# A decoder layer on one core: both feed-forward blocks as seven products of half-size blocks, the down projection in three passes

## The chip, the cores and the metric

One Trainium2 chip, one of its cores. The engines are TensorE (PE; its weight loads are listed as PEld), VectorE (DVE), ScalarE (ACT), GpSimd (POOL) and SyncE (SP, which here only issues DMAs). The metric is the device time of one execution in microseconds (us). The kernel before has three timed runs: 1122.57, 1123.95 and 1125.03 us, median 1123.95.

## The reference

One layer of a decoder, 512 tokens of 1024 float32 features. Cut to what matters:

```python
def swiglu(x, wg, wu, wd):
    return (jax.nn.silu(x @ wg) * (x @ wu)) @ wd

h = h + 0.5 * swiglu(rmsnorm(h, ffn1_norm), ffn1_wg, ffn1_wu, ffn1_wd)
...
h = h + 0.5 * swiglu(rmsnorm(h, ffn2_norm), ffn2_wg, ffn2_wu, ffn2_wd)
gate = sigmoid(rmsnorm(h, ple_gate_norm) @ ple_w_gate)
h = h + gate * rmsnorm(p @ ple_w_proj, ple_norm)
```

Between the two feed-forward blocks stand a projection, two attention mixers and an output projection. `wg` and `wu` are 1024 x 2816, `wd` is 2816 x 1024. All weights are float32.

## The kernel before, in words

**Numbers in two parts.** TensorE multiplies float32r, which holds fewer digits than float32. So each operand is kept as two float32r parts, `hi` (a ScalarE copy) and `lo` (VectorE: the source minus `hi`), and each product of K tile by K tile is three matmuls (`passes`, L443): hi hi, hi lo, lo hi. Weights are loaded raw into a tile `st` and split by `split` (L355) into the tiles `hi` and `lo`.

**A feed-forward block** is `ffn` (L536). The 22 tiles of 128 hidden units go in chunks of 8, 7 and 7. In a chunk, gate and up of one tile take 8 K tiles x 3 matmuls each of 128 x 512 (hidden units by all 512 tokens), with the weights as the stationary operand; `hidden` (L449) makes silu(gate) x up and splits it. Then the chunk's rows of `wd` are multiplied for each half of 512 output columns and each of the 4 token tiles, and the sum is added to `h` with one VectorE op per token tile and half. That is 22 x 48 = 1056 matmuls for gate and up and 22 x 24 = 528 for down, in each block.

**The first block's start** is `ffn_start` (L471): the first two hidden tiles go K tile by K tile as `x` arrives, on a not yet normalized, transposed x; `rms_rows` (L517) then makes 1/rms as a row, and `hidden` multiplies gate by that row. The other tiles follow at once on the same `xT`. In the second block, `norm_tok` (L423) norms and transposes each token tile as it is finished, and the products of the embedding (`embedding`, L1153) stand between.

**What sets the order.** The program is recorded by `Plan` and issued by a list schedule (`issue`, L206): each engine takes, of the recorded instructions that are ready by the planner's cost estimates (`cost`, L107), the earliest. All instructions are therefore of line L296 in the profile (`emit`), and are told apart by their tiles. Each engine runs its list strictly in order. Tiles of a tag share a fixed number of slots (`Tag`); a tile of most tags (`x8`, `pt`, `k4`, `hi`, `lo`, `st`) gets a slot only in program order; `w2`, and the PSUM tags `acc` and `gub`, may go ahead. All loads and stores of size are issued by SP's queue. A cost is estimated from an instruction's engine, operation and size.

**Names in the profile.** `gub` and `acc` are PSUM banks (4 each), `w` is a `w2` tile of 512 columns, `k` a `k4` tile of 1024, `x` an `x8` tile of 2048, `pt` one of 1664; `hl`, `s`, `r` and `cs` are small tiles of the mixing.

Of the kernel before, what the change touches and what calls it, by code (L numbers as in the profile page):

```python
# [20 lines left out]
K4 = 14  # L21
# [33 lines left out]
class Plan:  # L55
    """Records the program and issues it in the order of a list schedule: each engine takes, of the
    instructions whose operands and slots are there, the one that stands first in the program."""
# [25 lines left out]
    def box(self, ap):  # L83
        """The partitions and, as a bit mask, the words of each partition that ap covers."""
# [104 lines left out]
    def weave(self, *streams, weights=None):  # L189
        """Records the streams side by side, in step by their work on the tensor engine."""  # L190
# [15 lines left out]
    def issue(self):  # L206
# [14 lines left out]
        def slot(op):  # L221
            """When the new tiles of op can have their slots; None if not yet known."""
# [14 lines left out]
        while done < len(ops):  # L237
# [18 lines left out]
            if best is None:  # L256
                raise RuntimeError("schedule stuck at " + str(oldest))
# [41 lines left out]
class Layer:  # L299
# [18 lines left out]
    def w2(self, shape=(P, 512), dt=F32):  # L318
        return self.nc.tile(self.sb, shape, dt, "w2", 8, 3)
# [7 lines left out]
    def act(self, m):  # L327
        """[128, 2, 512]: the two parts of one tile of hidden units, the m-th of its chunk."""
        if m < 4:
            return self.pt()[:, :1024].rearrange("p (a c) -> p a c", a=2)  # L330
        return self.k4((P, 2, 512), F32R)

    def pt(self):
        return self.nc.tile(self.sb, (P, 1664), F32R, "pt", 4)

# [19 lines left out]
    def split(self, st, a, n, gain=None, step=0, lo_engine=None):  # L355
        """st [128, a, n] as its two float32r parts."""
# [15 lines left out]
    def gain_columns(self, names, after=()):  # L372
        """Gains as columns, [128, K tiles] each."""
# [19 lines left out]
    def rstd(self, ss, n, cols=1):  # L393
        """(ss / n + eps) ** -0.5"""
# [10 lines left out]
    def transposed(self, srcs, dst_hi, dst_lo, gain=None):  # L405
        """Up to four [128, 128] blocks transposed, times their gain columns, and split into the two parts."""
# [31 lines left out]

    def new_xT(self):
# [8 lines left out]

    def hidden(self, m, pg, pu, R):  # L449
        """silu(gate * R) * up, in two parts."""  # L450
        nc = self.nc
        sg, a32 = self.w2(), self.w2()
        if R is not None:
            nc.vector.tensor_mul(sg, pg, R)
            pg = sg
        nc.scalar.activation(sg, pg, AF.Silu)
        nc.vector.tensor_mul(a32, sg, pu)
        at = self.act(m)
        nc.scalar.copy(at[:, 0], a32)
        nc.vector.tensor_sub(at[:, 1], a32, at[:, 0].bitcast(F32))  # L460
        return at[:, 0], at[:, 1]
# [881 lines left out]
```

## Time and profile before

| what | value |
|---|---|
| timed runs | 1122.57, 1123.95, 1125.03 us |
| median | 1123.95 us |
| span of the profiled execution, first to last instruction | 1122.3 us |
| instructions in the profile | 15134 |
| DMA over the span | 106.60 MB, mean 95 GB/s |

The profile is one execution. The page gives its span alone and no time of its own around it; the median of the timed runs is 1.65 us above the span. Busy time of an engine is the union of its instructions' records. Matmuls are pipelined, so one record (some 390 ns for 512 columns) is longer than the distance from one matmul to the next; a rate is read from the start of a run to its end, divided by the number of matmuls. In a timeline, instructions of one kind that follow each other are merged to one row with their count (x2) and their length together; a bracket tells how long the engine was idle before, and what ended that.

### The profile page before, as it was taken

The page shows a single profiled execution, that of the slowest core. Times are in us where ns is not written, and L with a number is a line of the kernel's source. Part 1 is how long each engine was busy: PE and PEld are TensorE (multiplying, and loading weights), DVE is VectorE, ACT ScalarE, POOL GpSimd, SP SyncE. Part 2 cuts the span into 40 slices and gives each one's busy share as a digit, 9 for nine tenths or more (in the row PEclk, how much of TensorE's full clock was granted, in tenths as well). Part 3 has the DMA queues.
Part 4 walks back from the last instruction along what each step waited for, and adds up shares of the span by engine and source line. Part 5 has one row for each costly group of instructions (what it writes and reads, how often), then busy time and mean ns, then how long its engine had stood idle before and what let it go on. Part 6 is the DMA issues. An engine that isn't in the chain of part 4 may idle for free.

```text
span 1122.3 us, 15134 instructions
## 1 busy us (share of the span) xinstructions
PE 1106.8 (99%) x5635; PEld 941.9 (84%) x5635; DVE 587.6 (52%) x1121; ACT 493.9 (44%) x1017; POOL 161.7 (14%) x312
## 2 busy tenths in 40 slices
PE   9999999999999999999999999999999999999998
PEld 6888888888888988898999888888888888888887
DVE  5443343334443687889889887733333323333353
ACT  5332132222321767978988964522222221222252
POOL 2000000000000167553344511200000000000010
PEclk9999999999999999999999999999999999999999
DMA  7432333333343631312102232433223323332221
GB/s 215 123 97 94 94 94 95 100 88 112 95 107 84 213 119 39 76 30 58 36 25 72 100 125 73 137 103 102 94 75 113 94 85 103 104 103 85 90 80 66
DMA packets 143657, 106.60 MB, mean 95 GB/s; under 512 B 12624, under 2 KB 125296, under 8 KB 143584
## 3 DMA queue, kind: packets, MB, share of 16 engines
q1 hardware_dynamic: 143392, 105.55, 31.3%
q8 instruction: 45, 0.74, 0.3%
q14 instruction: 28, 0.23, 0.1%
q0 software_dynamic: 192, 0.08, 0.1%
HBM read 101.29 MB, written 4.33 MB: 94 GB/s over the span
## 4 chain that ended last, share of the span: by engine, by line
PE 87%; DVE 4%; POOL 2%; ACT 2%; issue 2%; DMA 1%; SPq 0%; POOLq 0%; ACTq 0%
PE gub L296 49%; PE acc L296 39%; DVE k L296 1%; POOL s L296 1%; ACT w L296 1%; DVE w L296 1%; POOL r L296 1%; POOL w L296 1%; ACT k L296 1%; DVE s L296 1%; DVE lo L296 0%; DMA st<-in_w_in 0%; DVE x L296 0%; DMA spill<-k 0%; DMA ident<-in_ident 0%
## 5 line engine op out<-in xcount | busy, mean ns | idle before, releaser
L296 PE MATMUL gub<-x,hi 128*128 128x512 f32 x1376 | 424.7, 390 | 0.0
L296 ACT CAST hi<-st 128x1024 fp32r<-128x1024 f32 (+4 forms) x171 | 166.1, 981 | 502.4 <-PE acc L296 181.6
L296 PEld LDWEIGHTS gub<-x,hi 128*128 128x128 f32 x1376 | 258.3, 188 | 53.1
L296 DVE TENSOR_TENSOR lo<-st,hi 128x1024 fp32r<-128x1024 f32 (+4 forms) x171 | 192.6, 1134 | 194.4 <-ACT hi L296 189.7
L296 PE MATMUL gub<-x,lo 128*128 128x512 f32 x688 | 267.8, 389 | 0.0
L296 PE MATMUL acc<-hi,x 128*128 128x256 f32 (+3 forms) x720 | 181.9, 329 | 0.0
L296 PE MATMUL acc<-hi,k 128*128 128x512 f32 (+1 forms) x512 | 166.0, 391 | 2.2 <-DVE k L296 2.0
L296 PEld LDWEIGHTS gub<-x,lo 128*128 128x128 f32 x688 | 129.2, 188 | 26.9
L296 POOL TENSOR_SCALAR s<-s 128x1 f32<-128x1 f32 (+3 forms) x65 | 18.6, 286 | 801.6 <-ACT k L296 755.9
L296 PEld LDWEIGHTS acc<-hi,x 128*128 128x128 f32 x720 | 123.3, 190 | 5.2
L296 PE MATMUL acc<-hi,pt 128*128 128x512 f32 x384 | 122.4, 395 | 0.0
L296 PE MATMUL acc<-lo,x 128*128 128x256 f32 (+3 forms) x360 | 117.5, 328 | 0.0
L296 PEld LDWEIGHTS acc<-hi,k 128*128 128x128 f32 x512 | 96.7, 190 | 19.8 <-issue 2.2
L296 PE MATMUL acc<-lo,k 128*128 128x512 f32 (+1 forms) x272 | 103.2, 383 | 0.0
L296 DVE TENSOR_TENSOR w<-w,gub 128x512 f32<-128x512 f32 x42 | 28.9, 688 | 135.6 <-PE gub L296 135.6
L296 PEld LDWEIGHTS acc<-hi,pt 128*128 128x128 f32 x384 | 72.3, 188 | 16.9
L296 PE MATMUL acc<-lo,pt 128*128 128x512 f32 x192 | 75.7, 394 | 0.0
L296 PEld LDWEIGHTS acc<-lo,x 128*128 128x128 f32 x360 | 68.2, 190 | 2.7
L296 ACT ACTIVATE w<-w,s 128x128 f32<-128x128 f32 (+1 forms) x96 | 53.8, 563 | 9.7 <-DVE s L296 9.3
L296 PEld LDWEIGHTS acc<-lo,k 128*128 128x128 f32 (+1 forms) x272 | 50.0, 184 | 8.5
L296 PE MATMUL gub<-ident,w 128*128 128x128 f32 (+2 forms) x316 | 52.4, 274 | 0.6 <-ACT w L296 0.2
L296 POOL TENSOR_TENSOR s<-s,mhalf 128x1 f32<-128x1 f32 (+3 forms) x61 | 49.4, 810 | 4.1
(154 smaller groups left out, 1198.9 us busy)
## 6 DMA issues: line engine op xcount, KB each, us to landing
st<-in_ffn_wg SPq DMA_DIRECT2D x42, 512.0 KB, 3.8
st<-in_ffn_wu SPq DMA_DIRECT2D x42, 512.0 KB, 3.9
st<-in_ffn_wd SPq DMA_DIRECT2D x40, 512.0 KB, 3.6
st<-in_w_in SPq DMA_DIRECT2D x48, 128.0 KB, 2.5
st<-in_w_in SPq DMA_DIRECT2D x8, 512.0 KB, 3.8
st<-in_w_out SPq DMA_DIRECT2D x8, 512.0 KB, 3.8
st<-in_ple_w_gate SPq DMA_DIRECT2D x8, 512.0 KB, 3.9
k<-in_x SPq DMA_DIRECT2D x16, 128.0 KB, 4.1
```

The lines of the kernel that those rows point to most:

```text
L296: getattr(getattr(self.nc, op.eng), m)(*a, **k)
```

## The change

Gate and up, for two hidden tiles at a time (a pair), are a product of a 2 x 2 block matrix of weights (K halves by hidden tiles) with a 2 x 2 block matrix of x (K halves by token halves). The change computes it with seven products of half-size blocks instead of eight, after Strassen and Winograd: sums of blocks of x are made once per block in `x_operands`, sums of blocks of the weights for every pair in `gate_up`. Each of the seven products is 2 (gate, up) x 4 K tiles x 3 = 24 matmuls of 128 x 256. The first pair of the first block is still done as before. The hidden units stay in `k4` tiles, 11 of them.

The down projection comes after all pairs, and it too has seven products, 66 matmuls of 128 x 512 each; they don't fit in PSUM together, so it goes over all pairs three times: products 5, 6 and 4, then 1, 7 and 3, then product 2, whose sum goes on in the banks of product 1. Tokens 256 to 511 are finished after the second pass, 0 to 255 after the third, and the stages behind take the token tiles in the order 2, 3, 0, 1. The embedding's result, which stood in `x8` tiles through the second block, is written to DRAM and loaded again at the end.

The diff, cut to its core (V is VectorE, G is GpSimd):

```diff
-K4 = 14
+K4 = 17
+W2 = 9
...
-            return f * max(m / 1.2, self.cols(outs[0]) / 2.4) + 2.5
+            return f * max(m / 1.2 + 2.5, self.cols(outs[0]) / 2.4 + 13.5)
...
+        XR = [self.pt().bitcast(F32)[:, :1024].rearrange("p (k c) -> p k c", k=2) for _ in range(NK // 2)]
...
+            nc.gpsimd.tensor_tensor(XR[kp], xT[kp][0].bitcast(F32), xT[kp][1].bitcast(F32), ALU.add)
...
+    def two_parts(self, hi, lo, src):
+        nc = self.nc
+        nc.scalar.copy(hi, src)
+        nc.vector.tensor_sub(lo, src, hi.bitcast(F32))
+
+    def x_operands(self, XR, row=None):
...
+        if row is not None:
+            for x in XR:
+                for i in range(2):
+                    G.tensor_tensor(x[:, i], x[:, i], row, ALU.mult)
...
+                y = self.x8((P, 2, 4, 256))
+                hi, lo = y[:, 0], y[:, 1]
+            for n, a in enumerate(halves):
+                self.two_parts(hi[:, 2 * n:2 * n + 2], lo[:, 2 * n:2 * n + 2], a)
...
+        B = lambda r, c: [XR[2 * r + n][:, :, 256 * c:256 * c + 256] for n in range(2)]
...
+        sub(V, T3, B(1, 1), B(0, 1))
+        sub(G, T, B(0, 1), B(0, 0))
+        operand(7, T3)
+        operand(5, T)
+        sub(G, T, B(1, 1), T)
+        operand(6, T)
+        operand(1, B(0, 0))
+        sub(G, T, B(1, 0), T)
+        operand(4, T)
+        operand(2, B(1, 0))
+        operand(3, B(1, 1))
...
+    def gate_up(self, p, X, wg, wu):
...
+        for n, (r, c) in enumerate(((0, 0), (1, 0), (1, 1), (0, 1))):
+            t = self.st() if n % 2 else self.pt().bitcast(F32)[:, :1024]
...
+        s3 = self.pt().bitcast(F32)[:, :1024].rearrange("p (g k c) -> p g k c", g=2, k=4)
+        G.tensor_tensor(flat(s3), flat(q[0, 0]), flat(q[1, 0]), ALU.subtract)
+        w7 = operand(s3)
+        s = q[1, 0]
+        V.tensor_tensor(flat(s), flat(s), flat(q[1, 1]), ALU.add)
+        w5 = operand(s)
+        rc, rb, rd, r1 = self.gub(), self.gub(), self.accb(), self.accb()
+        product(7, w7, rc, True, False)
+        G.tensor_tensor(flat(s), flat(s), flat(q[0, 0]), ALU.subtract)
+        w6 = operand(s)
+        product(5, w5, rb, True, False)
+        p5 = self.w2()
+        nc.scalar.copy(p5, rb)
+        c22 = self.w2()
+        V.tensor_tensor(c22, p5, rc, ALU.add)
+        w1 = operand(q[0, 0])
+        product(6, w6, rd, True, True)
+        V.tensor_tensor(flat(s), flat(q[0, 1]), flat(s), ALU.subtract)
+        w4 = operand(q[1, 1])
+        product(1, w1, r1, True, False)
+        z = self.w2()
+        nc.scalar.copy(z, r1)
+        V.tensor_tensor(z, z, rd, ALU.add)
+        V.tensor_tensor(c22, c22, z, ALU.add)
...
+    def down(self, h, acts, wd, on_token):
...
+        steps = [range(a, min(a + 2, n)) for a in range(0, n, 2)]
...
+        b5, b6, b4 = [[f(), f()] for f in (self.accb, self.accb, self.gub)]
+        for st in steps:
...
+                w = self.x8((P, 4, 512), F32)
+                nc.sync.dma_start(w[:].rearrange("p (a d) c -> p a d c", a=2), raw(p))
+                G.tensor_tensor(w[:, 1], w[:, 1], w[:, 0], ALU.subtract)
+                V.tensor_tensor(w[:, 3], w[:, 3], w[:, 1], ALU.subtract)
+                G.tensor_tensor(w[:, 2], w[:, 2], w[:, 3], ALU.subtract)
...
+                G.tensor_tensor(s[:, 0], a[:, 2], a[:, 3], ALU.add)
+                G.tensor_tensor(s[:, 1], s[:, 0], a[:, 1], ALU.subtract)
+                o = act_op(3)
+                self.two_parts(o[:, 0, 0:2], o[:, 1, 0:2], s)
+                self.two_parts(o[:, 0, 2], o[:, 1, 2], a[:, 3])
+                V.tensor_tensor(a[:, 2], a[:, 1], a[:, 2], ALU.subtract)
+                V.tensor_tensor(a[:, 3], a[:, 0], s[:, 1], ALU.subtract)
+                acs.append(o)
+            for i, (banks, slot) in enumerate(((b5, 1), (b6, 3), (b4, 2))):
+                w = operands([x[:, slot] for x in ws])
+                for tt in range(2):
+                    product(banks, acs, i, w, first, last, tt)
+        for tt in range(2):
+            t = self.w2()
+            nc.scalar.copy(t, b5[tt])
+            V.tensor_tensor(t, t, b6[tt], ALU.add)
+            add(2 + tt, 0, b6[tt])
+            add(2 + tt, 0, b4[tt])
+            add(tt, 1, t)
+            add(2 + tt, 1, t)
...
+                G.tensor_tensor(w[:, 1], w[:, 2], w[:, 1], ALU.subtract)
...
+                self.two_parts(o[:, 0], o[:, 1], acts[p][:, 1:4])
...
+            nc.scalar.copy(t, b1[tt])
+            V.tensor_tensor(u, t, b7[tt], ALU.add)
+            add(2 + tt, 0, u)
+            add(2 + tt, 1, u)
+            on_token(2 + tt)
+            V.tensor_tensor(t, t, b3[tt], ALU.add)
+            add(tt, 1, t)
...
-    xT = L.new_xT()
+    XR = [L.pt().bitcast(F32)[:, :1024].rearrange("p (k c) -> p k c", k=2) for _ in range(NK // 2)]
...
     next(emb)
+    X = L.x_operands(XR)
     next(emb)
-    e = next(emb)
+    spilled, e_r = next(emb)
```

`norm_raw`, new, is `norm_tok` with plain copies of the transposed parts to `XR` in place of the split.

## Rows read from the trace of the kernel before

**Rows 1.** The page: busy time of each engine; its busy tenths in 40 slices.

```profile
PE 1106.8 (99%) x5635; PEld 941.9 (84%) x5635; DVE 587.6 (52%) x1121; ACT 493.9 (44%) x1017; POOL 161.7 (14%) x312
...
POOL 2000000000000167553344511200000000000010
```

**Rows 2.** Chain of waits in order of time: start, length, what.

```profile
100.05 44.09 PE acc L296 x192
144.13 76.17 PE gub L296 x336
...
704.74 4.78 PE acc L296 x21
```

**Rows 3.** Stretches: length, busy PE, PEld, DVE, ACT, POOL, clock, DMA share, GB/s.

```profile
402.00:406.00 4.00, 3.54 (x18) 3.57 (x19) 4.00 (x11) 1.95 (x5) 3.57 (x6) 0.61 0.05 14
5.00:10.00 5.00, 5.00 (x18) 3.07 (x17) 2.17 (x4) 2.58 (x5) 0.00 (x0) 1.00 0.98 316
144.00:220.00 76.00, 76.00 (x337) 62.96 (x336) 31.43 (x35) 21.73 (x27) 0.00 (x0) 1.00 0.33 100
```

**Rows 4.** Timeline of PE in the projections: start, length, operation, out<-in, shape, count.

```profile
396.18 0.28 PE L296 MATMUL acc<-lo,x 128*128 128x256 f32 x1
...
400.13 0.28 PE L296 MATMUL acc<-lo,x 128*128 128x256 f32 x1
402.46 0.35 PE L296 MATMUL acc<-hi,k 128*128 128x256 f32 x1 [2.05 <-DVE k L296]
```

**Rows 5.** Groups by line and form: count, busy us, mean ns, idle before.

```profile
L296 DVE TENSOR_TENSOR lo<-st,hi 128x1024 fp32r<-128x1024 f32 x134 | 163.6, 1224 | 184.0 <-ACT hi L296 179.2
L296 ACT CAST hi<-st 128x1024 fp32r<-128x1024 f32 x134 | 140.8, 1054 | 474.1 <-PE acc L296 172.3 <-PE gub L296 158.1 <-issue 139.0
L296 DVE TENSOR_TENSOR lo<-st,hi 128x512 fp32r<-128x512 f32 x16 | 10.6, 686 | 1.9 <-ACT hi L296 1.9
L296 DVE TENSOR_TENSOR w<-w,s 128x256 f32<-128x256 f32 x8 | 3.5, 438 | 2.6 <-POOL s L296 2.5
L296 POOL TENSOR_TENSOR w<-w 128x256 f32<-128x256 f32 x16 | 11.3, 705 | 16.8 <-ACT w L296 16.8
L296 POOL TENSOR_TENSOR x<-x,w 128x512 f32<-128x512 f32 x8 | 10.4, 1303 | 19.3 <-DVE w L296 14.5 <-PE gub L296 4.8
L296 POOL TENSOR_TENSOR r<-w,sin 128x16 f32<-128x16 f32 x24 | 7.9, 348 | 0.0
```

**Rows 6.** Timelines of DVE and POOL in the mixing, three places.

```profile
404.24 0.28 DVE L296 TENSOR_TENSOR k<-w,k 128x128 fp32r<-128x128 f32 x1
405.32 1.28 DVE L296 TENSOR_TENSOR lo<-st,hi 128x1024 fp32r<-128x1024 f32 x1
405.48 1.42 POOL L296 TENSOR_TENSOR r<-w,sin 128x16 f32<-128x16 f32 x2
...
539.20 1.29 POOL L296 TENSOR_TENSOR x<-x,w 128x512 f32<-128x512 f32 x1
539.49 1.22 DVE L296 TENSOR_TENSOR pt<-gub,pt 128x512 fp32r<-128x512 f32 x3 [0.36 <-ACT pt L296]
...
622.45 1.28 POOL L296 TENSOR_TENSOR x<-x,w 128x512 f32<-128x512 f32 x1 [0.18 <-DVE w L296]
622.95 0.93 DVE L296 TENSOR_TENSOR k<-w,k 128x128 fp32r<-128x128 f32 x1
```

**Rows 7.** Timelines of DVE, PE and ACT at the start of block one.

```profile
8.58 1.29 DVE L296 TENSOR_TENSOR lo<-st,hi 128x512 fp32r<-128x512 f32 x2 [0.21 <-ACT hi L296]
...
33.77 0.77 PE L296 MATMUL acc<-ident,w 128*128 128x128 f32 x5
34.69 0.58 ACT L296 COPY k<-acc 128x512 f32<-128x512 f32 x1
```

**Rows 8.** Timeline of DVE at the start of block two: the last token's parts.

```profile
705.22 1.28 DVE L296 TENSOR_TENSOR x<-gub,x 128x512 fp32r<-128x512 f32 x2
```

More of the change, by code (lines that the diff above doesn't have):

```diff
@@ L256, in issue @@
             if best is None:
-                raise RuntimeError("schedule stuck at " + str(oldest))
+                o = ops[oldest]
+                raise RuntimeError(f"schedule stuck at {oldest}: {o.eng} {o.call[0]} {o.tiles} "
+                                   + str({n: (len(t.free), t.queue[t.head:t.head + 2]) for n, t in self.tags.items()}))
             t, op = best
@@ new lines, in pair_tile, with operand, product, hidden @@
+    def pair_tile(self):
+        return self.k4((P, 4, 256))
+    def gate_up(self, p, X, wg, wu):
+        nc = self.nc
+        V, G = nc.vector, nc.gpsimd
+        q = {}
+        for n, (r, c) in enumerate(((0, 0), (1, 0), (1, 1), (0, 1))):
+            t = self.st() if n % 2 else self.pt().bitcast(F32)[:, :1024]
+            q[r, c] = t.rearrange("p (g k c) -> p g k c", g=2, k=4)
+            for i, w in enumerate((wg, wu)):
+                view = w[512 * c:512 * c + 512, (2 * p + r) * P:(2 * p + r + 1) * P]
+                nc.sync.dma_start(q[r, c][:, i], view.rearrange("(k p) c -> p k c", p=P))
+        flat = lambda x: x.rearrange("p g k c -> p (g k c)")
+        def operand(src):
+            hi, lo = self.hilo((P, 2, 4, P))
+            self.two_parts(flat(hi), flat(lo), flat(src))
+            return hi, lo
+        def product(i, w, bank, first, last):
+            for g in range(2):
+                for k in range(4):
+                    for n, (a, b) in enumerate(self.passes([x[:, g, k] for x in w], [x[:, k] for x in X[i]])):
+                        nc.tensor.matmul(bank[:, 256 * g:256 * g + 256], lhsT=a, rhs=b,
+                                         start=(first and g == k == n == 0), stop=(k == 3 and n == 2),
+                                         skip_group_check=True)
+        s3 = self.pt().bitcast(F32)[:, :1024].rearrange("p (g k c) -> p g k c", g=2, k=4)
[22 more added lines that the diff above has]
+        V.tensor_tensor(c22, c22, z, ALU.add)
+        acts = self.pair_tile()
+        def hidden(c, slot):
+            sg = self.w2()[:, :256] if c.space == PSUM else c[:, 0:256]
+            nc.scalar.activation(sg, c[:, 0:256], AF.Silu)
+            V.tensor_tensor(acts[:, slot], sg, c[:, 256:512], ALU.mult)
+        hidden(c22[:], 3)
+        w2 = operand(q[0, 1])
+        product(4, w4, rc, False, True)
+        c21 = self.w2()
+        V.tensor_tensor(c21, z, rc, ALU.add)
+        hidden(c21[:], 0)
+        w3 = operand(s)
+        product(2, w2, r1, False, True)
+        hidden(r1[:], 1)
+        product(3, w3, rb, False, True)
+        c12 = z
+        V.tensor_tensor(c12, z, rb, ALU.add)
+        hidden(c12[:], 2)
+        return acts
@@ L621, in mix_consts, with project @@
         self.lf = c("lf", (P, NT, 8))
-    def project(self, xT, groups, done, name):
+    def project(self, xT, groups, done, name, order=range(NT)):
         nc, d = self.nc, self.d
@@ L638, in project @@
         yield
-        for t in range(NT):
+        for t in order:
             ps = self.accb()
@@ L1164, in embedding @@
         yield
-        es, ss = [], [self.small(2) for _ in range(NT)]
+        spill = [self.dram.tile([P, NT, 512], F32, name=f"spill_e{half}") for half in range(2)]
+        ss = [self.small(2) for _ in range(NT)]
         for half in range(2):
             w = self.wcols(wp, 0, half)
-            e = self.x8((P, NT, 512), F32)
-            es.append(e)
             for t in range(NT):
@@ L1182, in embedding @@
             nc.gpsimd.tensor_tensor(s1, ss[t][:, 0:1], ss[t][:, 1:2], ALU.add)
-            r = self.rstd(s1, D)
-            for half in range(2):
-                e = es[half][:, t]
-                nc.vector.scalar_tensor_tensor(e, e, r, g[:, half * 512:half * 512 + 512], op0=ALU.mult, op1=ALU.mult)
-        yield es
+            r.append(self.rstd(s1, D))
+        yield spill, r
 @with_exitstack
@@ L1201, in layer @@
     w1 = d["ffn1_wg"][0], d["ffn1_wu"][0]
[L1202 to L1203 removed]
+    XR, started = L.ffn_start(x, h, L.gcol["ffn1_norm"], *w1)
+    row = L.rms_rows(h)
+    X = L.x_operands(XR, row)
+    first = L.started_acts(started, row)
     spill = [L.dram.tile([P, D], F32, name=f"spill{t}") for t in range(NT)]
     L.gain_columns(["mix_norm", "ple_gate_norm", "out_norm_nsa", "out_norm_fox"], [L.started])
[L1206 removed]
+    aT, a_r = [], [None] * NT
     def to_mix(t):
@@ L1282, in layer @@
     ks = [L.xk(gT[0], k) for k in range(NK)]
+    e = [L.x8((P, NT, 512), F32) for _ in range(2)]
+    ge = gain("ple_norm")
     for half in range(2):
+        nc.sync.dma_start(e[half], spilled[half])
+        for t in range(NT):
+            nc.vector.scalar_tensor_tensor(e[half][:, t], e[half][:, t], e_r[t], ge[:, half * 512:half * 512 + 512],
+                                           op0=ALU.mult, op1=ALU.mult)
         w = [L.wcols(wg, kp, half, L.gcol["ple_gate_norm"]) for kp in range(4)]
-        for t in range(NT):
-            step = 256 if half and t == NT - 1 else 512
+        for t in (2, 3, 0, 1):
+            step = 256 if half and t == 1 else 512
             for c in range(0, 512, step):
```

219 lines of the change are left out of this document (128 added, 91 removed).

## The prediction

> **What bounds the kernel now.** I read the share of busy time per engine first: TensorE is busy for 1106.8 of 1122.3 us, VectorE for half the span, and POOL (GpSimd) for 161.7 us [rows 1]. The slices say where: POOL has work at the start and in the middle (the mixing) and shows 0 in the stretches of the two feed-forward blocks [rows 1]. The chain of waits is there one run of products after another, each beginning where the last ends [rows 2]: 192 products of 512 columns in 44.09 us in a down projection, or 229.6 ns each, and in gate and up 336 in 76.17 us, or 226.7 ns. A table of stretches shows what lies beside the products of gate and up: VectorE 31.43 of 76 us, ScalarE 21.73, POOL nothing, DMA busy a third [rows 3]. So TensorE bounds both blocks, and only fewer columns, or the same columns faster, can gain there; whatever else gets slower than TensorE takes its place.
>
> **What the change takes away.** A product of 256 columns is not in the blocks now, but in the projections: from 396.18 to 400.13 us stand 33 of them, 119.7 ns each [rows 4]; I use 120. Gate and up: the first block keeps its first two tiles as they are, so 20 + 22 tiles change. Before, 42 x 48 = 2016 products x 226.7 ns = 457.0 us; after, 21 pairs x 168 = 3528 x 120 = 423.4 us; 33.6 us less. Down: 7/8 of 528 products in each block, 132 fewer in both, x 229.6 ns = 30.3 us less. Together **63.9 us less TensorE work**. In the rows a product takes its columns at 2.4 GHz plus 13.4 ns. [...]
>
> **What it adds.** Each operand of a product must be summed and then split into two parts. The prices: the split of 1024 columns costs ScalarE 1.05 and VectorE 1.22 us, of 512 VectorE 0.69; a 256-column op costs VectorE 0.44; POOL takes 0.70 for 256 and 1.30 for 512 [rows 5]. POOL at 1024 is not in the trace: at least 1.30, at most four times the 256 row, 2.8; the step from 256 to 512, 0.60, continued gives 2.5, which I take.
>
> These engines are not independent. While VectorE made a 1024-column split from two SBUF tiles (405.32 to 406.60), POOL's 16-column op, begun at 405.48, and the next one were not done until 406.90, though the group's mean is 348 ns. At 622.45 it is the other way: POOL's 512-column sum runs to 623.73, and VectorE's 128-column op on two SBUF tiles, begun at 622.95, ends at 623.88, 0.93 us for what the same op takes in 0.28 at 404.24. At 539.20 POOL's sum ran beside three VectorE ops that read PSUM, and these took their usual time [rows 6]. So a POOL sum and a VectorE op with both inputs in SBUF **take turns**. [...] It speaks against this change, which gives POOL sums of SBUF tiles where it had none, beside splits that all read two SBUF tiles. So I add the times of the two engines wherever both work from SBUF.
>
> *Gate and up, per pair.* VectorE: 9 ops of 1024 (7 splits, 2 sums), 5 sums of 512, 4 products of 256. By means 9 x 1.22 + 5 x 0.69 + 4 x 0.44 = 16.2 us; back to back (two 512 splits in 1.29, so the second adds 0.60 [rows 7]) nearer 15. POOL: 2 x 2.5 = 5. Four of the 512 sums and one 256 product read PSUM and may run beside POOL. That is 19.9 to 21 us against 168 x 0.12 = 20.2 us of TensorE: just about full. ScalarE has 7 x 1.05 + some 3 = 10. Loads are 2 MB a pair as before. I take 0.4 us a pair: **8 us** (0 to 20).
>
> *Down, first pass, per pair.* TensorE: 18 x 0.2296 = 4.13 us. VectorE: 5 ops of 512 and 3 of 256, all from SBUF: 4.8 by means, 4.1 back to back. POOL: 2 of 512 and 2 of 256: 4.0, or 3.2 if a waiting op's fixed part hides. In turns: 7.3 to 8.8; I take the middle, 8.0, twice TensorE's need. Eleven pairs: 88 us. Ahead of the pass TensorE is still in the last gate-and-up pair, where the weights of up to six pairs may be loaded as the `x8` tiles come free, the first after 1/7 of that pair's 20 us; a load of 1 MB needs over 3 us at the 316 GB/s that the trace shows at full share [rows 3], and the pair's own last splits stand in the queue, so I take that 8 us of this work go before (0 to 12). 88 - 8 - 11 x 4.13 = 34.6: **34 us a block** (23 to 46), 68 in both.
>
> *Pass two:* VectorE 3 splits of 512 and one of 768, POOL one 512 sum: about 4.1 us a pair, level with TensorE. But VectorE enters it late and with 2 x 5 evacuation ops (512 columns, as 0.69) ahead of the new operands in its queue: **7 us a block** (4 to 16), 14. *Pass three:* no POOL sums; VectorE has 2 x 5 evacuation ops, the 4 splits of two tokens' norms and 11 pairs x (0.69 + 0.44), some 7 + 3 + 12 = 22 us against 66 x 0.23 = 15.2, part of it done before: **5 us a block** (2 to 8), 10.
>
> *Start of block one.* Now the products of the third tile follow the first two at once. After the change everything must first become an `x_operands` tile. The row of 1/rms is there at 35.3 (transposes at 33.77 behind the first products, ScalarE's copy at 34.69 [rows 7]). Then POOL multiplies 8 x 1.30 = 10.4: 45.7. The new pair's third `pt` tile, `s3`, needs a slot that an `XR` tile holds until the sums for operands 7, 6 and 4 and the split for 2 have read it, and the `x8` tiles go in strict order, so 7, 5, 6, 1 and 4 come before 2: POOL 5 x 1.30 and VectorE 12 x 0.69 in turns, 14.8: 60.5. Then the other half on POOL 1.3, `s3` 2.5, its split 1.05 + 1.22, and hand-overs: about 67.3, against the end of the transposes at 34.5 [rows 7]. **33 us** (20 to 40; at the low end the engines overlap), and no other product is in reach. q00 and q11 load meanwhile, once operand 1 is split.
>
> *Start of block two.* The same from the last token's parts, now ready at 706.5 [rows 8], without the multiplications: 5 x 1.30 + 13 x 0.69 = 15.5, then 1.3 + 2.5 + 2.3: 728. The embedding's products cover TensorE until 709.5 [rows 2]. 18 us; the first half of that work can begin with the first tiles: **16 us** (5 to 22).
>
> *Clock.* After an idle 2.05 us before 402.46 [rows 4] the granted clock of 402 to 406 is 0.61 [rows 3], against 1.00 elsewhere: some 3.1 of 4 us at the lower level, 1.2 GHz, half of which is lost, 1.5 us. Two long idles and some in the passes: **4 us** (3 to 10).
>
> *At nothing:* the stores of e (8 x 256 KB) and its later load; SP's queue has room, DMA moves under a third of the time in the blocks [rows 3], against 316 GB/s at full share there. Its eight multiplications move from the second block's start to the end, where VectorE waits for products; if that cover fails, 8 x 0.69 = 5.5 us. Loads in pass one, 11.5 MB in 80 us, are 144 GB/s. The new token order (2, 3, 0, 1) lets the project and the gate begin on finished tokens while 0 and 1 are normed. The planner's new costs reorder the mixing: 0, within 5 either way.
>
> **Sum.** 8 + 68 + 14 + 10 + 33 + 16 + 4 = 153 added, 63.9 removed: 1122.3 + 89.1 = 1211.4 for the span. The page gives the profiled execution's span alone; the median of the runs is 1.65 above it and I take that as what lies around: **1213 us**.
>
> **Rivals.** (a) *Sharing costs nothing, faster.* If POOL's sums ran beside VectorE's, pass one would ask 4.8 of VectorE and 4.0 of POOL against 4.13: 6 us a block with the evacuations; gate and up would fit; the starts would be 26 and 12, as their chains still wait in turn for slots; clock 3. 53 - 63.9 = 11 less: 1113. It decides at a first pass of 4.13 us a pair. Against it stand both blocked ops of [rows 6]; for it, that these are narrow ops. Chance 0.09. (b) *The sharing costs its low end,* 7.3 a pair with 12 us done ahead (23 a block), gate and up level, starts 25 and 10, passes two and three 8 a block, clock 3: 100 added: 1160. Chance 0.15. (c) *Gate and up fall behind too:* 1 us a pair (21) and pass one at 8.8 without a head start longer than 8 (43 a block), the rest as forecast (77): 184 added: 1244. Chance 0.12. (d) The sums of (a) and (b) mix to no change; 0.02. That the change doesn't do what it says is excluded on TensorE by the 120 ns.
>
> **Chances.** The forecast has 0.62, and its own range is 1180 to 1245. With (b) and most of (c): 1150 to 1255. Faster by over 0.2% (2.2 us, about what a measurement of this kernel can tell) 0.09, within it 0.02, slower 0.89.
>
> **What would show it.** In the profile after: POOL busy in the blocks; VectorE's 512 splits in pass one longer than 0.69 in the mean, as each waits for a POOL sum; TensorE's busy share of pass one near a half, waiting for VectorE's `lo`; an idle TensorE of some 30 us after the first products and 16 at the second block's start; a gate-and-up pair every 20.2 to 21 us. The prediction is wrong if pass one takes less than 6 us a pair, or if products of the first new pair begin before 50 us.

## The result, and the profile after

The changed kernel takes **1199.87 us** (median of 4 runs, 1198.95 to 1200.68), the kernel before 1124.03 beside it (4 runs, 1122.57 to 1125.03): ratio 1.0678, 95% interval 1.0662 to 1.0693. Slower, as forecast, and 13 us less so than the 1213 predicted. The span of its profiled execution is 1198.6 us, 76.3 more than before.

The page after: busy time of each engine, then the 40 slices of POOL and of the granted clock.

```profile
PE 1073.9 (90%) x7015; PEld 971.7 (81%) x7015; DVE 1026.6 (86%) x1599; ACT 662.0 (55%) x1350; POOL 502.2 (42%) x484
...
POOL 5632222548723156653434510732323276754000
...
PEclk9589999999889999999999999799999999989999
```

Against [rows 1]: TensorE's share falls from 99 to 90%, VectorE's rises from 52 to 86%, and POOL, which showed zeros in both blocks, works through them.

The table of stretches cuts the span where the kind of product changes. Columns as in [rows 3]. In order: the start of block one, its gate and up (10 pairs), its first and second pass of down, the mixing, the start of block two, its gate and up (11 pairs), its first and second pass.

```profile
33.00:63.10 30.10, 0.01 (x1) 0.00 (x0) 23.81 (x23) 12.01 (x20) 22.90 (x15) 0.53 0.18 52
63.10:276.50 213.40, 204.55 (x1681) 203.65 (x1682) 200.83 (x199) 100.34 (x140) 81.00 (x41) 0.98 0.38 111
276.50:345.00 68.50, 54.29 (x200) 40.32 (x199) 62.94 (x76) 28.62 (x56) 46.85 (x28) 0.90 0.44 161
345.00:394.60 49.60, 47.09 (x200) 38.17 (x199) 42.77 (x62) 27.80 (x50) 14.01 (x6) 0.97 0.43 121
...
415.60:759.00 343.40, 327.21 (x2141) 295.22 (x2138) 276.20 (x736) 257.45 (x697) 148.79 (x268) 1.00 0.25 74
759.00:775.40 16.40, 0.05 (x2) 0.01 (x1) 14.02 (x18) 8.87 (x19) 13.84 (x13) 0.59 0.50 150
775.40:1009.60 234.20, 226.74 (x1848) 225.63 (x1849) 219.47 (x217) 110.78 (x154) 90.14 (x47) 0.97 0.37 111
1009.60:1078.40 68.80, 53.10 (x201) 39.10 (x200) 64.24 (x79) 29.59 (x60) 46.57 (x29) 0.93 0.47 170
1078.40:1128.30 49.90, 47.08 (x200) 38.14 (x199) 41.87 (x57) 26.84 (x47) 14.24 (x6) 0.97 0.29 96
```

Set each length against its products alone. A pair is 168 x 0.12 = 20.16 us, so gate and up should take 201.6 and 221.8: they are 11.8 and 12.4 late. A pass is 198 products; at 226.7 ns, 44.9: the first passes lose 23.6 and 23.9 us, the second 4.7 and 5.0. TensorE idles through the starts, 30.1 and 16.4 us, and VectorE is busy 92 to 94% of gate and up and of the first passes. The mixing, which the diff touches only at its edges, takes 343.4 us; the stretch that answers to it in the kernel before is this one:

```profile
376.70:709.40 332.70, 323.54 (x2148) 297.24 (x2147) 277.70 (x742) 260.61 (x701) 143.80 (x270) 0.99 0.26 76
```

It is 10.7 us shorter, with the same products and nearly the same clock (0.99 and 1.00).

The chain of waits (start, length, what) in block two:

```profile
811.07 3.11 PE gub L299 x24
...
831.29 2.85 PE gub L299 x24
...
851.26 2.85 PE gub L299 x24
...
956.51 2.52 POOL st L299
959.04 0.89 POOL w L299
959.95 0.95 DVE k L299
...
974.00 4.45 PE gub L299 x24
...
987.05 4.77 DMA x<-in_ffn_wd
991.95 2.24 POOL x L299
```

A PE row of 24 on `gub` is product 4, the fifth of a pair (7, 5, 6, 1, then 4). In the middle of the block these come 20.2 and 20.0 us apart, as runs of products that follow each other, like [rows 2]. Towards its end the chain leaves TensorE. `POOL w` and `DVE k` at 959 are sums of hidden units, `DMA x<-in_ffn_wd` and `POOL x` at 987 a load and a sum of down's weights: the first pass is being prepared in the queues that the last two pairs still need, and TensorE waits. In block one POOL has then made 21 of the pass's 44 sums (its groups from 226 to 276.4 us):

```profile
L299 POOL TENSOR_TENSOR x<-x 128x512 f32<-128x512 f32 x5 | 9.8, 1977 | 9.4 <-DVE x L299 8.9 <-DMA x<-in_ffn_wd 0.5
L299 POOL TENSOR_TENSOR w<-k 128x256 f32<-128x256 f32 x8 | 9.3, 1166 | 0.0
L299 POOL TENSOR_TENSOR w<-w,k 128x256 f32<-128x256 f32 x8 | 8.4, 1061 | 0.3
```

Not all of the lateness stands there. From first product to first product, the last two pairs take 23.2 and 27.0 us in block one and 24.5 and 25.6 in block two, but the first pairs take 23.4 and 23.7 as well, and the pairs between them 20.0 to 20.7. TensorE starts each first pair, behind the idle start, at a granted clock of 0.50: in block one, from 65.24 to 68.65 us, 16 products start 213 ns apart, and not 120 (columns as above):

```profile
63.10:69.10 6.00, 5.04 (x22) 4.74 (x23) 2.94 (x3) 1.61 (x2) 2.36 (x1) 0.50 0.30 88
...
775.40:782.50 7.10, 6.63 (x29) 6.34 (x30) 2.46 (x3) 2.00 (x3) 5.87 (x6) 0.50 0.32 97
```

The first pass of block one by groups (277 to 345 us; columns as in [rows 5]):

```profile
L299 DVE TENSOR_TENSOR lo<-x,hi 128x512 fp32r<-128x512 f32 x33 | 32.4, 1018 | 1.3 <-ACT hi L299 1.3
...
L299 POOL TENSOR_TENSOR x<-x 128x512 f32<-128x512 f32 x22 | 40.9, 1874 | 19.9 <-DMA x<-in_ffn_wd 9.7 <-DVE x L299 8.7 <-DVE pt L299 1.5
...
L299 PE MATMUL acc<-lo,pt 128*128 128x512 f32 x44 | 20.0, 454 | 10.6 <-DVE lo L299 10.6
```

VectorE's split of 512, 686 ns in [rows 5], takes 1018 in the mean; POOL's sum of 512, 1303 there, takes 1874; and TensorE waits for `lo`. The timeline shows what a mean of 1874 is made of (POOL first, then VectorE):

```profile
299.80 1.65 POOL L299 TENSOR_TENSOR x<-x 128x512 f32<-128x512 f32 x1 [0.63 <-DVE x L299]
...
308.55 8.17 POOL L299 TENSOR_TENSOR x<-x 128x512 f32<-128x512 f32 x1 [3.70 <-DVE x L299]
...
300.24 1.49 DVE L299 TENSOR_TENSOR pt<-k,pt 128x256 fp32r<-128x256 f32 x1
...
309.00 1.28 DVE L299 TENSOR_TENSOR lo<-x,hi 128x512 fp32r<-128x512 f32 x2
310.20 0.41 DVE L299 TENSOR_TENSOR k<-k 128x256 f32<-128x256 f32 x1
...
313.69 1.88 DVE L299 TENSOR_TENSOR lo<-x,hi 128x512 fp32r<-128x512 f32 x3
319.26 2.38 DVE L299 TENSOR_TENSOR x<-x 128x512 f32<-128x512 f32 x2 [3.69 <-POOL x L299]
```

At 300.24 a VectorE split of 256, 0.41 us in the mean of E1, where POOL is idle, takes 1.49 beside POOL's sum. At 308.55 it is the other way, and worse: VectorE has a full queue until 315.57, and POOL's sum, 1.30 us in [rows 5], lasts 8.17 us, until 316.72. Its next sums then run while VectorE, now with an empty queue, waits 3.69 us for them. Each engine stands still for the other in turn, as [rows 6] showed in small.

The ends of the two idle starts, on PE's timeline:

```profile
63.13 0.80 PE L299 MATMUL gub<-x,hi 128*128 128x256 f32 x2 [30.13 <-ACT hi L299]
...
775.39 0.79 PE L299 MATMUL gub<-x,hi 128*128 128x256 f32 x2 [16.35 <-ACT hi L299]
```

### The profile page after: what moved, and what is told of

Same layout as the page of the kernel before. It is cut to its first block, busy times and chain, and to the rows that moved or that the text cites. A ratio compares the mean times of both kernels' runs of the same rounds, so it can differ in the third digit from the quotient of the medians.

```text
span 1198.6 us, 19312 instructions
## 1 busy us (share of the span) xinstructions
PE 1073.9 (90%) x7015; PEld 971.7 (81%) x7015; DVE 1026.6 (86%) x1599; ACT 662.0 (55%) x1350; POOL 502.2 (42%) x484
## 5 line engine op out<-in xcount | busy, mean ns | idle before, releaser
L299 PE MATMUL gub<-x,hi 128*128 128x256 f32 x1008 | 191.4, 291 | 58.4 <-ACT hi L299 47.9
L299 PEld LDWEIGHTS gub<-x,hi 128*128 128x128 f32 x1008 | 162.2, 197 | 60.6 <-ACT hi L299 49.0
L299 PE MATMUL acc<-x,hi 128*128 128x256 f32 x1008 | 181.6, 282 | 0.0
L299 POOL TENSOR_TENSOR x<-x 128x512 f32<-128x512 f32 x66 | 129.7, 1981 | 86.5 <-DMA x<-in_ffn_wd 49.2
L299 PEld LDWEIGHTS acc<-x,hi 128*128 128x128 f32 x1008 | 154.9, 189 | 0.0
L299 PE MATMUL acc<-x,lo 128*128 128x256 f32 x504 | 141.8, 282 | 4.3 <-DVE lo L299 4.3
L299 PE MATMUL gub<-x,lo 128*128 128x256 f32 x504 | 145.7, 289 | 0.0
L299 ACT CAST hi<-x 128x512 fp32r<-128x512 f32 (+1 forms) x140 | 84.8, 642 | 103.8 <-PE acc L299 62.9
L299 DVE TENSOR_TENSOR lo<-x,hi 128x512 fp32r<-128x512 f32 (+1 forms) x140 | 120.2, 896 | 11.8 <-ACT hi L299 11.8
L299 DVE TENSOR_TENSOR lo<-pt,hi 128x1024 fp32r<-128x1024 f32 x63 | 115.1, 1826 | 8.4 <-ACT hi L299 8.4
L299 PEld LDWEIGHTS acc<-x,lo 128*128 128x128 f32 x504 | 94.9, 189 | 4.7 <-DVE lo L299 4.7
L299 ACT CAST hi<-pt 128x1024 fp32r<-128x1024 f32 x63 | 65.9, 1048 | 51.0 <-PE acc L299 30.3
```

Of the source, the lines that this page charges most:

```text
L299: getattr(getattr(self.nc, op.eng), m)(*a, **k)
```

## The experiments

| kernel | median, us | ratio to the kernel before (95%) |
|---|---|---|
| the changed kernel | 1199.87 | 1.0678 (1.0662 to 1.0693) |
| E1 down's sums on VectorE | 1170.25 | 1.0422 (1.0399 to 1.0445) |
| E2 POOL fills in place of sums | 1127.46 | 1.0040 (1.0026 to 1.0054) |
| E3 XR in k4 slots | 1188.61 | 1.0579 (1.0563 to 1.0595) |
| E4 seven products in gate and up only | 1148.75 | 1.0225 (1.0210 to 1.0240) |
| E5 seven products in down only | 1152.79 | 1.0260 (1.0244 to 1.0277) |
| E6 kernel before, new matmul estimate | 1134.31 | 1.0096 (1.0081 to 1.0111) |
| E7 changed kernel, old matmul estimate | 1190.54 | 1.0593 (1.0576 to 1.0611) |
| E8 gate and up of block two only | 1130.64 | 1.0064 (1.0049 to 1.0079) |
| E9 E8, old estimate, start covered | 1120.29 | 0.9973 (0.9964 to 0.9982) |
| E10 E9 and block one, covered | 1115.00 | 0.9931 (0.9918 to 0.9943) |
| E11 E10, parts further apart | 1115.67 | 0.9930 (0.9918 to 0.9943) |
| E12 E1, E3 and E7 together | 1148.29 | 1.0222 (1.0206 to 1.0237) |

My theory was **turns**: POOL's sums and VectorE's two-operand ops exclude each other. The rivals were a VectorE that is simply too slow, with POOL free beside it, and a chain of waits through POOL.

**E1, the sums on VectorE.** In `down` alone:

```diff
-                G.tensor_tensor(w[:, 1], w[:, 1], w[:, 0], ALU.subtract)
+                V.tensor_tensor(w[:, 1], w[:, 1], w[:, 0], ALU.subtract)
...
```

> The changed kernel with the five sums a pair that GpSimd makes for the down projection moved to VectorE. Three theories of the 23 us that each first pass takes beyond its matmuls, and of the 12 us by which the last two pairs of gate and up are late. Turns (a GpSimd sum and a VectorE operation that reads two SBUF operands exclude each other, so that their times add): a pair needs 10 us of both engines now, 5.3 of them GpSimd's (3 sums of 1.30, 2 of 0.70) and 4.7 VectorE's; on VectorE alone the five sums take 2.6 us, so a pair needs some 6.7 to 7.3 us of one engine against 4.1 us of matmuls. Faster than the changed kernel, by 15 to 40 us: 1160 to 1185. VectorE alone is too slow and GpSimd works free beside it: 2.6 us more in each of 22 pairs, slower by 30 to 57 us: 1230 to 1257. A chain of waits (load, sum, sum, split) sets the pace: VectorE's sums are shorter than GpSimd's, so faster too, but then VectorE's splits of 512 columns stay at their mean of 1.0 us and it stands idle between them, where by the turns they fall to 0.69 or less and it has no idle time.

29.6 us faster than the changed kernel, by giving *more* work to the engine that looked overloaded. First pass, stretch and VectorE's group (270 to 327 us):

```profile
270.00:327.00 57.00, 49.25 (x201) 38.85 (x200) 54.81 (x108) 27.94 (x53) 0.00 (x0) 0.94 0.52 190
...
L299 DVE TENSOR_TENSOR lo<-x,hi 128x512 fp32r<-128x512 f32 x32 | 19.9, 680 | 0.0
```

VectorE has 108 ops in place of 76 and is busy for less time, 54.8 us against 62.9; the split is back at 680 ns with no idle time before it. The slow-VectorE theory, which asked for 1230 or more, falls; so does the chain, by the length of the splits. VectorE now bounds the pass: 57.0 us against 44.9.

**E2, POOL busy without reading.**

```diff
+    def pool_writes(self, dst):
+        for _ in range(3):
+            self.nc.gpsimd.memset(dst, 0.01)
...
-                G.tensor_tensor(w[:, 1], w[:, 1], w[:, 0], ALU.subtract)
+                self.pool_writes(w[:, 1])
...
```

> The changed kernel with each of GpSimd's five sums a pair of the down projection replaced by three fills of the same destination with a constant: GpSimd stays busy at the same places in the same order of waits, but reads no SBUF operand. This leaves those sums out, so the down projection multiplies other numbers. Turns: VectorE's splits of 512 columns in the first pass fall from a mean of 1.02 us to 0.69 or less, 4.2 us of VectorE a pair stand against 4.1 of matmuls, and most of the excess of the first passes and of the late last pairs goes: faster than the changed kernel by 40 to 65 us, 1135 to 1160. VectorE alone too slow: the splits keep their length and nothing changes, within 5 us of 1200. A chain of waits through GpSimd: the splits are short but VectorE waits for the fills, and the time stays within 10 us of 1200 if three fills take as long as a sum.

1127.5, 72 us faster and below my range. First pass by stretch, then VectorE's and POOL's groups (268 to 312 us):

```profile
267.70:312.60 44.90, 44.90 (x201) 37.16 (x200) 39.51 (x73) 27.02 (x52) 33.44 (x79) 1.00 0.69 248
...
L299 DVE TENSOR_TENSOR lo<-x,hi 128x512 fp32r<-128x512 f32 x32 | 20.8, 680 | 3.1 <-ACT hi L299 3.1
...
L299 POOL MEMSET x<- 128x512 f32 x59 | 28.8, 530 | 11.4 <-DMA x<-in_ffn_wd 8.1 <-DVE lo L299 2.3 <-DVE k L299 0.5
```

TensorE is never idle: 44.9 us, exactly 198 products. Three fills (1.59 us by the mean) take POOL longer than a sum that is alone (1.30) and stand in the same places of its queue, so POOL's own time was not the cost. The fills also drop POOL's waits for VectorE's sums (8.7 us on `DVE x` in the rows of the changed kernel), so E2 alone doesn't part the reading from the waits. The instructions' own lengths do: VectorE's 73 ops take 39.5 us here, where 76 took 62.9, and that difference of 23.4 us is the 23.6 that the pass had lost. Two-operand ops beside POOL's reads were the cost, and E1, which keeps every wait and moves the sums, agrees. The DMA moves 248 GB/s here in place of 161, so the loads weren't it either. The other stretches say how far the loss reached: gate and up 204.5 and 225.1 us (late by 2.9 and 3.3 in place of 11.8 and 12.4), the second passes 46.1 (late by 1.2). Most of the lateness ahead of and behind the first pass was thus down's sums as well; what is left in gate and up is the first pair (23.7 and 23.3 us; the granted clock of the stretches is 0.98 and 0.99).

**E3, the slots of the start.**

```diff
-        XR = [self.pt().bitcast(F32)[:, :1024].rearrange("p (k c) -> p k c", k=2) for _ in range(NK // 2)]
+        XR = [self.k4((P, 2, 512)) for _ in range(NK // 2)]
...
```

> The changed kernel with the copy of x that the sums of x read (XR, four tiles) in slots of the tag k4 in place of pt, so that it no longer holds the four pt slots into which the first weight block q00 and the first sum of weights s3 of the Strassen pairs must go. Theory slot: the first products wait for q00, whose load goes out only when a pt slot comes free (54.7 us in block one), and for s3 behind it: idle falls from 30.1 to some 17 to 24 us in block one and from 16.4 to 5 to 10 in block two, 13 to 22 us faster, 1178 to 1187. Theory chain: the sums and splits of x (eight products by the row on GpSimd, four sums, fourteen splits) fill that time themselves: less than 5 us of change. Slower is possible if k4 slots, which the hidden units need, come free later than the pt slots.

The slot theory was right about the idle time and wrong about what it is worth: the time missed its range by 1.6 us. PE's timeline at the start of block one, and the stretch of gate and up behind it:

```profile
51.02 0.58 PE L299 MATMUL gub<-x,hi 128*128 128x256 f32 x1 [16.73 <-ACT x L299]
...
51.00:270.20 219.20, 206.82 (x1680) 204.69 (x1681) 210.00 (x208) 102.91 (x147) 86.07 (x46) 0.96 0.35 106
```

The idle falls from 30.1 to 16.7 us, and in block two the first product follows the mixing at once: 30 us less idle ahead of the first products. Yet only 11.3 us are gained. About 7 us a block come back inside the first pair: it takes 30.3 us in place of 23.4 in block one and 30.4 in place of 23.7 in block two, with TensorE waiting for operands that the idle start had given VectorE and ScalarE the time to make. Block one's gate and up so take 219.2 in place of 213.4. Its passes are longer too: the first and second by 0.9 each, the third by 3.9, where TensorE waits 1.6 for a split and then runs 3 us at a granted clock of 0.50. Block one's last product comes at 413.7 in place of 414.3: nearly all of its 13.4 us is given back. Block two keeps 10 of its 16.4, with gate and up 6.4 longer.

**E4 and E5, each half of the change alone.** E4 has `gate_up` with a plain down in one pass (eight banks, 528 products); E5 has the plain gate and up with the new `down`. Cores of both edits:

```diff
@@ E4, in down @@
+        for p in range(n):
+            w, tiles = load(p)
+            if p < n - 2:
+                for t in order:
+                    mm(t, p, w, tiles)
...
@@ E5, in ffn @@
-            acts.append(self.gate_up(p, X, wg, wu))
+                for k in range(NK):
+                    for i, (a, b) in enumerate(self.passes(w, self.xk(xT, k))):
+                        nc.tensor.matmul(ps, lhsT=a[:, k, :], rhs=b, start=(k == 0 and i == 0),
+                                         stop=(k == NK - 1 and i == 2))
...
```

> Gate and up as in the changed kernel, the down projection in plain products again: all 22 tiles in one pass over eight banks, 528 matmuls a block as before, with no sums on GpSimd and no third loads. If the late last pairs, the passes and their turns all belong to the seven-product down: the kernel before, less 33.6 us of matmuls of gate and up, with 46.5 us of idle starts and some 4 us of slower clock: 1136 to 1146, so still slower than before by 1 to 2 per cent, and the last pairs of gate and up at 20.2 us like the others. If gate and up fall behind by themselves: the last pairs stay late and the time is 1155 to 1170.

> Gate and up as in the kernel before (plain, tile by tile), the down projection with seven products in three passes as in the changed kernel. Down's matmuls save 30.3 us. By the turns (GpSimd's sums and VectorE's two-operand operations add, 10 us a pair against 4.1 of matmuls) the 35 us a block that gate-up's late last pairs and pass one lost together stay, less what more free VectorE time ahead of the first pass can hide, with 8 us of pass two and 3 of pass three: 1149 to 1175. If down's loss came from gate and up's own lack of free time instead, pass one falls back to some 46 us a block and the time is 1100 to 1115.

E4, gate and up and down of block one:

```profile
64.00:267.50 203.50, 202.54 (x1680) 202.25 (x1681) 189.31 (x185) 100.56 (x135) 53.74 (x19) 0.98 0.36 102
267.50:390.30 122.80, 122.80 (x556) 101.66 (x555) 46.80 (x74) 40.68 (x71) 2.23 (x6) 1.00 0.39 118
```

E5, gate and up and the first pass of block one:

```profile
33.80:252.00 218.20, 218.20 (x965) 180.64 (x964) 106.58 (x130) 59.47 (x76) 28.28 (x24) 1.00 0.32 96
252.00:316.00 64.00, 52.23 (x199) 39.95 (x198) 57.67 (x67) 27.32 (x52) 42.79 (x25) 0.89 0.59 217
```

In E4 gate and up are 1.9 us late in place of 11.8 (and 2.3 in place of 12.4 in block two), and the first pairs account for that (23.8 us in block one; 22.6 and 21.8 for the first two of block two). This settles whose lateness the last pairs had: seven-product gate and up fit, if nothing else is in their queues. E4 missed its range by 3 us, because I had not yet counted the mixing's 10.7. In E5 gate and up are not late at all and the first pass still loses 64.0 - 44.9 = 19.1 us (some 18 at the 232.8 ns at which its `pt` products stand): down loses by itself. The two halves together lose more than apart. Both have the longer mixing (343.0 and 345.0 us, so 10.3 and 12.3 more than before). Less that, E4 costs 25.5 - 10.3 = 15.2 us, E5 29.4 - 12.3 = 17.1, and the whole change 75.8 - 10.7 = 65.1: some 33 us come from the meeting of a gate and up that fills VectorE with a down that needs it.

**E6 and E7, the planner's line.** The diff has one line that computes nothing, the estimate of a matmul. E6 puts it into the kernel before, E7 takes it out of the changed one:

```diff
-            return f * max(m / 1.2, self.cols(outs[0]) / 2.4) + 2.5
+            return f * max(m / 1.2 + 2.5, self.cols(outs[0]) / 2.4 + 13.5)
```

> The kernel before with one line of the change alone: the planner's estimate of a matmul (128x512: 226.8 ns in place of 215.8). The mixing stage takes 343 us in the changed kernel and 333 before. Theory order: the estimate gives the mixing another order of instructions, which costs these 10 us: 1130 to 1136. Theory elsewhere (slots, order of the token tiles, the spilled embedding): within 3 us of 1123.3.

> The changed kernel with the planner's estimate of a matmul as before. Theory order: the mixing stage goes from 343 back to some 333 us: 1188 to 1192, if the feed-forward blocks keep their times. Theory elsewhere: the mixing stays at 340 to 346 us, and the time moves by what the blocks' own order changes, within 5 us of 1200.

The mixing of E6:

```profile
378.00:720.50 342.50, 328.37 (x2138) 295.45 (x2137) 279.13 (x741) 258.99 (x695) 141.54 (x266) 0.99 0.26 74
```

and of E7:

```profile
416.00:752.30 336.30, 325.43 (x2148) 296.14 (x2146) 277.15 (x737) 255.71 (x698) 146.57 (x270) 0.99 0.26 77
```

Alone, the line makes the kernel before 10.9 us slower, 9.8 of it in the mixing: an estimate that is nearer to the measured 226.7 ns gives a worse order. In the changed kernel it explains 7.1 of the mixing's 10.7 us (9.3 of the whole time); the other 3.6 stay with the change's slots and token order, which I didn't separate.

**E12, the causes as one sum.** E1, E3 and E7 in one kernel, no further edit.

> The changed kernel with three single edits together: the planner's estimate of a matmul as before (alone 9.3 us faster), XR in k4 slots (alone 11.3 faster) and down's sums on VectorE (alone 29.6 faster). If the three causes are separate terms of one sum: 1200 less 50, 1146 to 1154. If they share the same lack of VectorE time, the start that comes earlier is given back again: 1155 to 1165.

The three alone gained 29.6, 11.3 and 9.3, together 50.2; the kernel gained 51.6. The terms add, within the spread of the runs.

**E8 to E11, towards a version that beats both.** E8 keeps seven products only where E4 says that they fit, and only in block two; E9 also takes the old estimate, splits the x operands of products 1 and 2 (which are blocks of x, no sums) after the first two token tiles, starts the first pair with these products, and records the embedding behind them; E10 adds block one, whose second pair stays plain, so that TensorE has 21.8 us of products while x's operands are made; E11 changes a distance in E10's `pt` tiles.

```diff
@@ E9, in ffn @@
+        pair = self.gate_up(0, X, wg, wu, True)
+        next(pair)
+        next(parts)
+        next(pair)
+        next(emb)
+        next(emb)
...
@@ E10, in the first block's ffn @@
+        for m in range(4):
...
+            if m == 2:
+                X = self.x_operands_row(XR, row)
+            self.hidden(dst, *out, row)
+        for p in range(2, FF // (2 * P)):
+            acts.append(self.gate_up(p, X, wg, wu))
...
@@ E11, in down @@
-                y = self.pt()[:, :1024].rearrange("p (x i c) -> p x i c", x=2, i=2)
+                y = self.pt()[:, :1536].rearrange("p (x i c) -> p x i c", x=2, i=3)[:, :, :2]
```

> An attempt at a version faster than the kernel before: seven products for gate and up of the second block alone, with XR in k4 slots so that the first products do not wait; gate and up of the first block and both down projections plain (one pass over eight banks). 11 pairs save 18.5 us of matmuls; the start of block two costs some 0 to 6 us more than before by the run with XR in k4; the mixing costs 0 to 10 us more as in the changed kernel: 1106 to 1122, 1114 the likeliest. If VectorE's lack of free time in these pairs gives the rest back: 1122 to 1130.

> The run with seven products for gate and up of the second block alone (1130.6), with two edits: the planner's estimate of a matmul as before, and the start of block two covered: products 1 and 2, which need no sums of x, go first, their x operands are split as soon as tokens 0 to 255 are there, and the embedding's products (48 of 128x512, 10.9 us) are recorded behind the first pair's start, so that TensorE has them while VectorE makes the sums. If the planner's estimate is worth 9 to 11 us and the cover 6 to 12 us: 1107 to 1116, faster than the kernel before by 0.7 to 1.5 per cent. If the matmuls that are saved come back as VectorE's lag in the later pairs whatever the start: 1118 to 1123.

> The same, and in the first block too gate and up of 9 of the 11 pairs with seven products: the first two pairs are plain, and the second of them (21.8 us of matmuls) stands over the time in which the operands of x are made; the row's products are VectorE's instead of GpSimd's. If that covers the 30 us start: 9 pairs save 15 us, less 0 to 8 us of rest and lag: 5 to 15 us below the other attempt. If VectorE can't make the operands beside the plain pair, TensorE waits 8 us or more and nothing or a loss is left: 0 to 10 us above it.

> The attempt with both blocks covered, with the low part of the hidden units 768 words behind the high part in its pt tile in place of 512, nothing else. The down products of that attempt start every 232.6 ns on average where those of the first pass of the run with GpSimd's fills, which read pt tiles with 768 words between the parts, start every 226.7. If the distance between the parts does it: 528 matmuls a block by 5.9 ns, 3.1 us a block, 6 us faster: 1107 to 1111. If it is the tile's place or the turning between banks: 1114 to 1116, unchanged.

E8 missed both of its ranges, the second by 0.6 us: its mixing pays the planner's line (344.1 us), and its gate and up take 233.7 us for 221.8 of products. The first pair alone takes 30.5 of them, since VectorE makes its operands only then; from the fourth on every pair takes 20.16, so the loss is the uncovered start and not a lag that grows. E9 gained 10.3, about what the estimate alone would explain by E6, and fell into its second range. The traces part the gain: the mixing without the embedding's products is 7.1 us shorter, as in E7, and the rest up to the end of gate and up 3.5, so the cover is worth some 3.5 us of the 11.9 that E8 loses there. The pairs behind it don't lag, so the second range was met for another reason than the one given. E10 is 5.3 us below E9, at the low end of its range, and faster than the kernel before by 0.69%. Its gate and up of block one (9 pairs), its down, and its gate and up of block two behind the first products:

```profile
63.30:246.20 182.90, 177.90 (x1466) 177.29 (x1466) 163.84 (x171) 89.03 (x123) 45.54 (x17) 0.99 0.35 98
246.20:371.60 125.40, 125.40 (x554) 101.91 (x554) 46.89 (x73) 40.67 (x71) 2.23 (x6) 1.00 0.39 116
...
729.00:938.20 209.20, 209.20 (x1745) 209.14 (x1744) 184.23 (x194) 104.58 (x144) 62.38 (x32) 1.00 0.38 109
```

TensorE is full in the last two, with VectorE at 88% in the last: 1745 products in 209.2 us, 119.9 ns each, is what the saving rests on. E11 changed nothing (1115.67 against 1115.00).

## Why the prediction was right, and by which steps

**What held.** The direction, and its cause: POOL and VectorE in turns decide pass one. E2 stands for rival (a), "sharing costs nothing": 1113 by its sum, 1124 with the 10.7 us of the mixing, 1127.5 measured. That rival failed on its condition alone, which the changed kernel doesn't meet. The slow start of block one (33 us forecast, 30.1 measured, first product at 63.13 against 67.3) and of block two (16 and 16.4) came as worked out, and E3 shows the forecast's link, the `pt` slot behind `XR`: 13.4 of the 30.1 us, and all of the 16.4, go with it, though some 7 us a block come back in the first pair. Of the five signs named in advance three are there: POOL's work in the blocks, the longer splits, the two idle starts. A pair in the middle of a block takes 20.0 us, just under the 20.2 to 21 that were named, and the first and the last ones 23 to 27. TensorE's busy share near a half in pass one is not there: it is 79%, and the 198 products alone would be 66%, since the pass took 6.2 us a pair and not 8. That is close to the 6 below which the prediction called itself wrong.

**Where single terms were off.** The sum, +89.1 for the span, was 12.8 us too high (76.3 measured). That it came so near is in part luck, as errors of both signs cancelled: pass one cost what rival (b) gave it (23 a block), and gate and up what rival (c) gave them (21).

- *Pass one: 34 a block, measured 23.6 and 23.9*, and *gate and up: 8 us in both, measured 24.2.* One step failed, "I take that 8 us of this work go before". More went before (21 of POOL's 44 sums), and not for nothing: it stands in VectorE's and POOL's queues ahead of the last two pairs' splits, which had no time to spare. The two terms together were forecast at 76 and are 71.7; most of the error was the place. E4 (1.9 us late without down's sums) and E2 (2.9) show it. Of the 24.2, beyond the bound of 20, some 7 are the first pairs, which begin at a granted clock of 0.50; without them gate and up stand at 17.
- *The planner's new costs: "0, within 5 either way"*; measured 7.1 of the mixing's 10.7 (E7), and 9.8 in the kernel before (E6): beyond its own bound. The other 3.6 us, from the change's slots and token order, had no term either. No row of the trace before carried it: that the mixing has 333 us of tightly ordered work on four engines could be seen, but not which way another order would go.
- *Pass two: 14, measured 9.7. Pass three: 10, measured 7.8*: it runs from 394.6 to 414.3 and from 1128.3 to 1146.4, 19.7 and 18.1 us for 66 x 0.227 = 15.0. Both were mis-sized high. That the evacuations overlap more than the step assumed is likely, but no run shows it.
- *Clock: 4*, too low. At the two starts alone it costs some 6 us, half of what TensorE is busy for there: the first pairs take 3.4 and 3.7 more than those in the middle, with the granted clock at 0.50 for their first 6 and 7 us (5.04 and 6.63 of them busy). A product of 256 columns then takes 213 ns, or 1.2 columns a ns, as the step had it. In the first passes it is 0.90 and 0.93. All of this lies inside the stretches above, so it isn't counted again below.
- *Down's removed 30.3 us* were too few by about 2.7: the 229.6 ns of [rows 2] was a mean of two rates (see the last section), and the new passes run at 226.7 (E2: 198 in 44.9 us).

So the mechanism was right and the sizes shifted: -4.3 for gate and up with pass one, -2.5 for the starts, -4.3 for pass two, -2.2 for pass three, -4 for the clock (its cost is in the first of these), -2.7 for the rate, +10.7 for the mixing. That is -9.3 of the -12.8; the other 3.5 are not assigned.

## What to carry to other kernels

Before work is given to GpSimd "because it is idle", look at what VectorE does at that time: where POOL's ops read SBUF and VectorE's had both inputs there, the work wasn't parallel in this kernel (a sum of 1.30 us took 8.17, a split of 0.41 took 1.49), and the same sums on the busy VectorE were faster (E1: 29.6 us). A saving on the bounding engine is worth only what the next engine has free beside it in that very stretch; each half of this change fitted beside its old neighbour better than beside the other half (E4, E5). In a kernel whose order a planner makes, a changed cost estimate is a change of its own, and is run alone.

## What the runs showed of the hardware that I had not expected

**Who loses.** I had counted turns one for one. The sum that POOL began at 308.55 stayed blocked over the VectorE instruction then running and 13 more behind it, 8.17 us in all for a sum of 1.29 in [rows 6], and finished 1.15 us after the last of them. That the two exclude each other the row bears out, but the block lasted for a whole queue of VectorE's and not for one instruction. Fills by POOL left VectorE's splits at 680 ns (E2).

**The same product runs at two rates.** In the kernel before, 48 down products with the hidden units in `pt` tiles take 11.32 us and 48 with them in `k4` tiles 11.05 (less the last one's tail: 232.5 and 226.9 ns each). E10 and E11, all in `pt`, run at 232.4; E4, with the same code and the same tiles in `pt`, at 226.7. E11 excludes the distance between the two parts (512 or 768 words). Over all runs, the `pt` products stand 227 to 228 ns apart in the changed kernel, E1, E2, E4 and E7, and 232 to 233 in the kernel before, E3, E5, E6 and E8 to E12. The fast ones are exactly those whose `XR` stands in `pt` slots; what that changes for the product stays open. It is worth 3 us a block, and about what the first and second pass of E3 are longer by (0.9 us each). The products of 256 columns differ too: a pair in the middle of a block takes 19.96 us in the changed kernel and E4, and 20.16 in E8 to E11.
